# Two of ScalarE's scalings of a token tile placed behind the next tile's square and root

## The chip, the cores and the metric

The kernel runs on one core of one Trainium2 chip. The metric is the device time of one execution in microseconds (us). The kernel before takes 2104.73 us, the median of three runs (2103.9 to 2104.93).

The core has a matrix engine (TensorE, in the profile PE, with PEld for its weight loads), VectorE (DVE), ScalarE (ACT), GpSimd (POOL) and SyncE (SP). The last computes nothing here and issues transfers. ScalarE issues some transfers too; such an issue stands in ScalarE's own instruction order and appears in the trace as ACTq.

## The reference

The reference is one residual decoder block for 512 tokens of width 2048. The change touches only its last lines, in which the gated result of the feed-forward layer is added to the residual stream and the whole row of a token is normalised:

```python
x = x + g2 * jnp.einsum('bsf,fd->bsd', jax.nn.gelu(gate) * val, w_down[l])
return rms_norm(x, norm_final)

def rms_norm(x, g):
    xf = x.astype(jnp.float32)
    y = xf * lax.rsqrt(jnp.mean(xf * xf, axis=-1, keepdims=True) + EPS)
    return (y * g.astype(jnp.float32)).astype(x.dtype)
```

The norm needs the squares of all 2048 columns of a token before any column can be scaled.

## The kernel before

Nearly all of the kernel is one list of steps, each of which multiplies a 512 KB unit of weights. Every fp32 product is made of three matmuls on rounded halves of the operands. The tiles hold features on the 128 partitions and the 512 tokens along the row, up to the last group of the down projection.

The down projection gives 2048 output columns in four groups g = 0 to 3 of 512 columns. Groups 0 to 2 are done in the feature layout. They are added to the residual, weighted with the final norm's gain (`weigh`), transposed on TensorE (`turned`) and kept as `rows[t][g]`: 128 tokens by 512 columns for each of the four token tiles t = 0 to 3. Their sums of squares come from `partial_squares` (`part`). All of that is ready before the end.

Group 3 is computed by tokens, in `group_by_token`. Most of its weight units are multiplied for all four tiles in turn. The last three units are kept back, and their products (six half units, 18 matmuls a tile) are done tile by tile. After tile t's 18 matmuls, `finish(t, ps)` is called:

```python
for t in range(4):
    for m in range(2 * (n - tail), 2 * n):
        mm_h(ps[t], ws[base + m // 2][m % 2], t, lhs[ks[m]], False, m == 2 * n - 1)
    done(t, ps[t])
```

`finish` works so, for one tile (lines of the profile in brackets):

- VectorE multiplies the matmul result by the gate (L1101) and adds the residual (L1102). This is y, the last 512 columns of the row.
- ScalarE squares y and sums along the row into v, one number a token (L1103: an ACTIVATE and an ACTIVATION_READ_ACCUMULATOR).
- VectorE meanwhile multiplies y by the final gain (L1104) and then adds the other columns' mean square to v (L1105).
- ScalarE takes the root (`root`, L105).
- VectorE makes the reciprocal root r in four small instructions (`rsqrt_rest`, L110, L111, L112, L117).
- The four 512-column pieces of the row are multiplied by r and written to `out`, 256 KB each. Piece 3 is done by VectorE (L1110), and pieces 0, 1, 2 by ScalarE (L1112), in that order. In tile 3, VectorE also does piece 1.
- The write of piece 0 is issued by ScalarE, those of the other three by SyncE (L1113).

The instruction order on each engine is the order in which this code runs: an engine does nothing of tile t + 1 before its own part of tile t. When all is written, the end of the program (L1295) waits on SyncE until the writes have landed.

Of the kernel before, what the change touches and what calls it, by code (L numbers as in the profile page):

```python
# [15 lines left out]
P = 128  # L16
S = 512
# [33 lines left out]
def tile_block(ctx, tc, x_t, vec, w_ada, w_in, w_r, w_i, ws_t, w_out, w_up, w_us, w_dn, out):  # L51
    nc = tc.nc
    V, A, G, PE, SY = nc.vector, nc.scalar, nc.gpsimd, nc.tensor, nc.sync
# [7 lines left out]
    def sb(tag, bufs, shape=(P, S), dt=F32, pl=pool):  # L61
        count[0] += 1
        return pl.tile(list(shape), dt, name=f"{tag}_{count[0]}", tag=tag, bufs=bufs)
# [39 lines left out]
    def root(v):  # L103
        s = sb("rsq", 4, (P, 16))[:, :v.shape[1]]
        A.activation(s, v, AF.Sqrt)  # L105
        return s

    def rsqrt_rest(r, v, s, whole=True):
        t = sb("rsq", 4, (P, 16))[:, :v.shape[1]]
        V.reciprocal(s, s)  # L110
        V.tensor_tensor(out=t, in0=s, in1=v, op=MUL)  # L111
        V.tensor_tensor(out=t, in0=t, in1=s, op=MUL)  # L112
        if whole:
            V.tensor_scalar(out=t, in0=t, scalar1=-0.5, scalar2=1.5, op0=MUL, op1=ADD)
            V.tensor_tensor(out=r, in0=s, in1=t, op=MUL)
        else:
            V.scalar_tensor_tensor(out=r, in0=t, scalar=3.0, in1=s, op0=SUB, op1=MUL)  # L117
# [376 lines left out]
    for k in range(KT):  # L494
        if k % 2 == 0:
            both = pair(F32)
        t = both[:, k % 2, :]
# [27 lines left out]
    r = sb("rsr", 2, (P, 4))  # L525
# [569 lines left out]
    def finish(t, ps):  # L1095

        y = rows[t][3]
        q = sb("yl", 4, pl=room2[0])
        v = sb("rsr", 2, (P, 4))[:, 0:1]
        r = sb("rsr", 2, (P, 4))[:, 0:1]  # L1100
        V.tensor_tensor(out=q, in0=ps, in1=across["g2"], op=MUL)  # L1101
        V.tensor_tensor(out=y, in0=q, in1=y, op=ADD)  # L1102
        A.activation(ps, y, AF.Square, scale=D ** -0.5, accum_out=v)  # L1103
        V.tensor_tensor(out=q, in0=y, in1=across["gf"], op=MUL)  # L1104
        V.tensor_tensor(out=v, in0=v, in1=part[0][:, t:t + 1], op=ADD)  # L1105
        rsqrt_rest(r, v, root(v), False)
        for g in (3, 0, 1, 2):
            src = q if g == 3 else rows[t][g]
            if g == 3 or (g == 1 and t == 3):
                V.tensor_scalar(out=src, in0=src, scalar1=r, scalar2=None, op0=MUL)  # L1110
            else:
                A.activation(src, src, AF.Copy, scale=r)  # L1112
            (A if g == 0 else SY).dma_start(out[t * P:(t + 1) * P, g * S:(g + 1) * S], src)  # L1113

    for half in range(2):
        for g in range(4):
            ks = range(HF * half, HF * half + HF)
            srcs = [w_dn[half, g, u] for u in range(HF // 2)]
            if half == 0:
                group(srcs, ks, mm_w, act, down_done(g))  # L1120
            elif g < 3:
                group(srcs, ks, mm_w, act, last_done(g))
            else:
                group_by_token(srcs, ks, act, finish, 3)
# [174 lines left out]
```

## Time and profile before

| | us |
|---|---|
| median of three runs | 2104.73 |
| the profiled execution, its own time | 2104.92 |
| its span, first to last instruction | 2103.2 |
| TensorE matmuls busy | 2069.0 |
| VectorE busy | 1492.9 |
| ScalarE busy | 923.8 |
| last matmul ends | about 2092.3 |
| last scaling ends | about 2099.4 |

Positions are microseconds from the start of the span. The profiled execution's own time is 1.7 us more than its span. The profile lists instructions by engine with start and duration, says what an engine waited for, and follows the work that ended last back to its causes. Transfers have an issue (an instruction of the engine that issues) and a landing. The share of the 16 DMA engines that is busy in a stretch is given beside the rate in GB/s. A bracket at the end of an instruction's row holds the time for which its engine was idle before it, and what ended that.

### The profile page before, as it was taken

The numbers are of one execution on the slowest core, as the hardware profiler recorded it, in microseconds if no ns is written. First come the engines' busy times: TensorE is split into PE (matmuls) and PEld (weight loads), VectorE is DVE, ScalarE is ACT, GpSimd is POOL, SyncE is SP. The second block draws the span as 40 slices with busy tenths as digits, with TensorE's granted clock in tenths as the row PEclk, the third lists the DMA queues.
The fourth block names the chain that finished last, engine by engine and source line by source line (L and its number), as shares of the span: only waits on it lengthen the run. The fifth ranks groups of instructions, "written<-read, shape, count | busy, mean of one in ns | idle before, by whom it ended". The sixth has DMA issues, their size and how long they took to land.

```text
span 2103.2 us, 26309 instructions
## 1 busy us (share of the span) xinstructions
PE 2069.0 (98%) x10160; PEld 1727.6 (82%) x10160; DVE 1492.9 (71%) x1865; ACT 923.8 (44%) x1165; POOL 79.7 (4%) x100
## 2 busy tenths in 40 slices
PE   7999999999989999999999999999999999999997
PEld 4887777888868888888888888888888888888886
DVE  8999889788767888888888888888875223432333
ACT  5323666332234555555555555555553222322223
POOL 0000000000000000000000000000000000000000
PEclk9999999999999999999999999999999999999999
DMA  9977434589825677877877867767755334423222
GB/s 374 327 288 264 141 127 154 199 296 367 298 95 159 212 225 202 241 216 202 242 216 204 240 211 210 248 198 235 216 177 199 121 119 141 159 91 99 92 90 100
DMA packets 116061, 420.36 MB, mean 200 GB/s; under 512 B 14816, under 2 KB 14944, under 8 KB 103648
## 3 DMA queue, kind: packets, MB, share of 16 engines
q1 hardware_dynamic: 87280, 315.39, 42.6%
q0 software_dynamic: 12672, 46.14, 11.6%
q10 hardware_dynamic: 15984, 57.15, 7.9%
q8 instruction: 80, 1.31, 0.2%
q14 instruction: 45, 0.37, 0.0%
HBM read 397.66 MB, written 20.97 MB: 199 GB/s over the span
## 4 chain that ended last, share of the span: by engine, by line
PE 87%; DVE 7%; ACT 3%; issue 1%; DMA 1%; SPq 0%; ACTq 0%; DVEq 0%
PE mm L921 28%; PE mm L922 14%; PE mm L174 13%; PE mm L175 13%; PE mm L176 13%; DVE araw L212 2%; PE mm L181 1%; PE mm L183 1%; PE mm L182 1%; DVE wl L168 1%; DMA araw<-w_ada 1%; DVE xs L359 1%; PE sm L655 0%; DVE la L685 0%; DVE xs L734 0%
## 5 line engine op out<-in xcount | busy, mean ns | idle before, releaser
L163 ACT CAST wh<-raw 128x1024 fp32r<-128x1024 f32 x296 | 311.7, 1053 | 615.1 <-PE mm L175 443.1
L168 DVE TENSOR_TENSOR wl<-raw,wh 128x1024 fp32r<-128x1024 f32 x296 | 360.9, 1219 | 303.8 <-ACT wh L163 303.4
L921 PE MATMUL mm<-hp,wh 128*128 128x512 f32 x1408 | 499.5, 399 | 0.0
L174 PE MATMUL mm<-hp,wh 128*128 128x512 f32 x1184 | 469.0, 396 | 6.7 <-ACT hp L229 5.8
L175 PE MATMUL mm<-hp,wh 128*128 128x512 f32 x1184 | 463.6, 392 | 0.5 <-DVE hp L237 0.5
L176 PE MATMUL mm<-hp,wl 128*128 128x512 f32 x1184 | 462.8, 391 | 0.0
L922 PE MATMUL mm<-hp,wl 128*128 128x256 f32 x1408 | 395.4, 281 | 0.0
L921 PE MATMUL mm<-xs,wh 128*128 128x512 f32 x1056 | 375.1, 399 | 0.0
L921 PEld LDWEIGHTS mm<-hp,wh 128*128 128x128 f32 x1408 | 264.6, 188 | 66.1
L922 PE MATMUL mm<-xs,wl 128*128 128x256 f32 x1056 | 296.6, 281 | 0.0
L174 PEld LDWEIGHTS mm<-hp,wh 128*128 128x128 f32 x1184 | 223.7, 189 | 58.3 <-ACT hp L229 8.7
L922 PEld LDWEIGHTS mm<-hp,wl 128*128 128x128 f32 x1408 | 266.0, 189 | 0.0
L175 PEld LDWEIGHTS mm<-hp,wh 128*128 128x128 f32 x1184 | 223.6, 189 | 50.1 <-issue 2.4
L176 PEld LDWEIGHTS mm<-hp,wl 128*128 128x128 f32 x1184 | 223.6, 189 | 46.6
L168 DVE TENSOR_TENSOR wl<-rawb,wh 128x1024 fp32r<-128x1024 f32 x176 | 214.9, 1221 | 65.6 <-ACT wh L163 65.6
L921 PEld LDWEIGHTS mm<-xs,wh 128*128 128x128 f32 x1056 | 198.4, 188 | 49.6
L922 PEld LDWEIGHTS mm<-xs,wl 128*128 128x128 f32 x1056 | 199.5, 189 | 0.0
L163 ACT CAST wh<-rawb 128x1024 fp32r<-128x1024 f32 x176 | 185.2, 1052 | 23.9 <-PE mm L921 13.3
L212 DVE SCALAR_TENSOR_TENSOR araw<-araw,crow 128x2050 f32<-128x2050 f32 (+1 forms) x80 | 182.6, 2286 | 2.5 <-DMA araw<-w_ada 2.4
L950 POOL DMA_DIRECT2D raw<-w_us x88 | 75.9, 862 | 1240.8 <-DMA rawb<-w_us 457.8
L974 ACT COPY u<-mm 128x512 f32<-128x512 f32 x88 | 51.7, 587 | 161.5 <-PE mm L922 161.5
L168 DVE TENSOR_TENSOR wl<-t,wh 128x1024 fp32r<-128x1024 f32 x44 | 53.9, 1225 | 50.3 <-ACT wh L163 50.3
(233 smaller groups left out, 2106.3 us busy)
## 6 DMA issues: line engine op xcount, KB each, us to landing
rawb<-w_us SPq DMA_DIRECT2D x132, 512.0 KB, 6.8
araw<-w_ada SPq DMA_DIRECT2D x48, 1024.5 KB, 7.6
raw<-w_dn SPq DMA_DIRECT2D x96, 512.0 KB, 3.6
raw<-w_us SPq DMA_DIRECT2D x88, 512.0 KB, 6.2
raw<-w_us POOLq DMA_DIRECT2D x88, 512.0 KB, 7.3
araw<-w_ada SPq DMA_DIRECT2D x32, 1025.0 KB, 8.4
raw<-w_in ACTq DMA_DIRECT2D x59, 512.0 KB, 4.6
yl<-w_ada SPq DMA_DIRECT2D x16, 1024.5 KB, 5.4
```

Of the source, the lines that this page charges most:

```text
L163: A.copy(hi, raw)
L168: V.tensor_tensor(out=lo, in0=raw, in1=hi, op=SUB)
L174: PE.matmul(ps, w[0][:, cs], h[0], start=first, stop=False)
L175: PE.matmul(ps, w[0][:, cs], h[1], start=False, stop=False)
L176: return PE.matmul(ps, w[1][:, cs], h[0], start=False, stop=last)
L181: PE.matmul(ps, h[0][:, cs], w[0], start=first, stop=False)
L182: PE.matmul(ps, h[0][:, cs], w[1], start=False, stop=False)
L212: V.scalar_tensor_tensor(out=raw, in0=raw, scalar=1.0, in1=crow[:, :w], op0=MUL, op1=MUL, accum_out=mods[:, n:n + 1])
L921: PE.matmul(both, hi[:, cs], m, start=first, stop=False, skip_group_check=True)
L922: PE.matmul(ps[:, lower], lo[:, cs], m[:, 0, :], start=False, stop=last, skip_group_check=True)
L950: G.dma_start(o[name], w_us[f - PLAIN, i], accum_op=ADD)
L974: A.copy(t, o["x"])
```

## The change

The change rewrites the end of `finish`. In tiles 0 to 2 only pieces 3 (VectorE) and 2 (ScalarE) are scaled at once. The scalings of pieces 0 and 1, both ScalarE's, are put into a function that runs in the next tile, right behind that tile's root. Tile 3 runs tile 2's two late scalings behind its own root, and then all its own four pieces. The issuing engines change as well: ScalarE now issues the write of piece 2 (in tile 3 those of 0 and 2), and SyncE those of the others. v and r get a tag of their own with four buffers, where they had two shared ones, because r of a tile is read while the next tile's is made.

```diff
-        v = sb("rsr", 2, (P, 4))[:, 0:1]
-        r = sb("rsr", 2, (P, 4))[:, 0:1]
+        v = sb("rsf", 4, (P, 4))[:, 0:1]
+        r = sb("rsf", 4, (P, 4))[:, 0:1]
         V.tensor_tensor(out=q, in0=ps, in1=across["g2"], op=MUL)
         V.tensor_tensor(out=y, in0=q, in1=y, op=ADD)
         A.activation(ps, y, AF.Square, scale=D ** -0.5, accum_out=v)
         V.tensor_tensor(out=q, in0=y, in1=across["gf"], op=MUL)
         V.tensor_tensor(out=v, in0=v, in1=part[0][:, t:t + 1], op=ADD)
-        rsqrt_rest(r, v, root(v), False)
-        for g in (3, 0, 1, 2):
+        s = root(v)
+        if t:
+            late_parts.pop()()
+        rsqrt_rest(r, v, s, False)
+
+        def part_of(g, engine, queue):
             src = q if g == 3 else rows[t][g]
-            if g == 3 or (g == 1 and t == 3):
+            if engine is V:
                 V.tensor_scalar(out=src, in0=src, scalar1=r, scalar2=None, op0=MUL)
             else:
                 A.activation(src, src, AF.Copy, scale=r)
-            (A if g == 0 else SY).dma_start(out[t * P:(t + 1) * P, g * S:(g + 1) * S], src)
+            queue.dma_start(out[t * P:(t + 1) * P, g * S:(g + 1) * S], src)
+
+        def later():
+            part_of(0, A, SY)
+            part_of(1, A, SY)
+
+        if t < 3:
+            part_of(3, V, SY)
+            part_of(2, A, A)
+            late_parts.append(later)
+        else:
+            part_of(3, V, SY)
+            part_of(0, A, A)
+            part_of(1, V, SY)
+            part_of(2, A, A)
+
+    late_parts = []
```

## Rows read from the trace of the kernel before

**Rows 1.** The page: the span, and busy time with share and instructions by engine.

```profile
span 2103.2 us, 26309 instructions
PE 2069.0 (98%) x10160; PEld 1727.6 (82%) x10160; DVE 1492.9 (71%) x1865; ACT 923.8 (44%) x1165; POOL 79.7 (4%) x100
```

**Rows 2.** The chain that ended last, its last links: start, duration, engine, tile, line.

```profile
2094.37 1.33 ACT xs L1112 x2
2095.70 0.62 ACT mm L1103 x2
2097.56 0.73 ACT xs L1112
2098.69 0.72 ACT xs L1112
```

**Rows 3.** ScalarE in order of time, tiles 0 to 2 (start, duration; ACTq is an issue).

```profile
2081.49 0.60 ACT L1103 ACTIVATE mm<-xs 128x512 f32<-128x512 f32 x1 [4.48 <-DVE xs L1102]
...
2082.23 1.28 ACT L105 ACT_TABLE_LOAD   x1
...
2085.30 0.35 ACTq L1113 DMA_DIRECT2D out<-xs  x1
2085.70 1.34 ACT L1112 ACTIVATE xs<-xs,rsr 128x512 f32<-128x512 f32 x2 [0.43 <-ACT xs L1112]
2086.94 0.58 ACT L1103 ACTIVATE mm<-xs 128x512 f32<-128x512 f32 x1
...
2087.87 0.20 ACT L105 ACTIVATE rsq<-rsr 128x1 f32<-128x1 f32 x1 [0.22 <-DVE rsr L1105]
2088.89 0.72 ACT L1112 ACTIVATE xs<-xs,rsr 128x512 f32<-128x512 f32 x1 [0.81 <-DVE rsr L117]
...
2091.29 0.58 ACT L1103 ACTIVATE mm<-xs 128x512 f32<-128x512 f32 x1
```

**Rows 4.** VectorE in order of time, tiles 0 to 2.

```profile
2080.77 0.69 DVE L1102 TENSOR_TENSOR xs<-yl,xs 128x512 f32<-128x512 f32 x1
...
2085.66 0.69 DVE L1102 TENSOR_TENSOR xs<-yl,xs 128x512 f32<-128x512 f32 x1
...
2088.89 0.49 DVE L1110 TENSOR_SCALAR yl<-yl,rsr 128x512 f32<-128x512 f32 x1
2089.29 0.68 DVE L1101 TENSOR_TENSOR yl<-mm,xs 128x512 f32<-128x512 f32 x1
2090.01 0.69 DVE L1102 TENSOR_TENSOR xs<-yl,xs 128x512 f32<-128x512 f32 x1
```

**Rows 5.** TensorE in order of time: the last matmul of tile 3.

```profile
2091.86 0.39 PE L183 MATMUL mm<-wh,dp 128*128 128x512 f32 x1
```

**Rows 6.** ScalarE in order of time, the scalings of tile 3.

```profile
2097.56 0.72 ACT L1112 ACTIVATE xs<-xs,rsr 128x512 f32<-128x512 f32 x1 [0.81 <-DVE rsr L117]
2098.31 0.34 ACTq L1113 DMA_DIRECT2D out<-xs  x1
2098.69 0.72 ACT L1112 ACTIVATE xs<-xs,rsr 128x512 f32<-128x512 f32 x1 [0.42 <-ACT xs L1112]
```

**Rows 7.** SyncE's issues in order of time, tile 3: its first and its last.

```profile
2098.07 0.33 SPq L1113 DMA_DIRECT2D out<-yl  x1
...
2099.44 0.33 SPq L1113 DMA_DIRECT2D out<-xs  x1
```

**Rows 8.** Issues: KB each, us to landing; 2098.07, then 2099.44; then all sixteen.

```profile
out<-yl SPq DMA_DIRECT2D x1, 256.0 KB, 2.1
...
out<-xs SPq DMA_DIRECT2D x1, 256.0 KB, 2.7
...
DMA to landing us min/median/max: 2.0/2.2/3.1
```

**Rows 9.** A stretch of the end: busy time by engine, granted clock, DMA share, GB/s.

```profile
2099.00:2101.50 2.50, 0.00 (x0) 0.00 (x0) 0.00 (x0) 0.41 (x1) 0.00 (x0) 0.50 1.03 386
```

**Rows 10.** Waits of SyncE's queue from 2098: us in total, times, longest.

```profile
SPq L1295 <- DMA out<-xs: 1.9, 3, 0.7
```

## The prediction

> **What bounds the kernel now.** First read the page: TensorE is busy for 2069.0 of a span of 2103.2 us [rows 1]. The change touches nothing of that. It acts only behind the last matmul of a tile, and the last matmul of all ends at 2091.86 + 0.39 = 2092.25 [rows 5], so at most the 11 us from there to the end are at stake, 0.5% of the time. The second view is the chain that ended last: from 2094 on it consists of ScalarE's scalings and squares, one behind another without a gap [rows 2]. So the end is not set by TensorE. It is set by a loop over token tiles, and the third view, ScalarE and VectorE in order of time, shows the loop. Tile 1's square starts at 2086.94 and tile 2's at 2091.29 [rows 3]: 4.35 us a tile. Tile 2's y was ready before that: its addition ran from 2090.01 to 2090.70 [rows 4]. In tile 0, where ScalarE was idle, the square came 0.03 us behind the same addition (2080.77 + 0.69 = 2081.46 against 2081.49) [rows 3, 4]. So 2091.29 - 2090.73 = 0.56 us of each turn is the square waiting for two scalings of the tile before, while VectorE, which needs the root, stands still.
>
> The fourth view is the transfers. In tile 3 the four writes are issued between 2098.07 and 2099.44 [rows 7]. The first lands 2.1 us later, at 2100.17, and the last 2.7 us later, at 2102.14 [rows 8]. Between 2099 and 2101.5 the 16 DMA engines are fully busy, at 386 GB/s [rows 9]. One write of 262144 bytes is 0.68 us at that rate, and the landings agree: (2102.14 - 2100.17) / 3 = 0.66. So the end is a stream of four writes. It begins when the first is issued, and the program's end waits for its last [rows 10].
>
> **The change part by part.**
>
> *The square comes forward.* Tile 1's addition ends at 2085.66 + 0.69 = 2086.35 [rows 4], so its square can start at 2086.38. ScalarE has to be free by then. After r of tile 0 it now does one scaling and one issue, where the row after the issue starts at 2085.70 [rows 3]; that is in time. From square to square the new loop is: square to the next use of r by VectorE, 2088.89 - 2086.94 = 1.95; that to the next gate multiplication, 2089.29 - 2088.89 = 0.40; that to the end of the addition, 2090.01 - 2089.29 + 0.69 = 1.41; and 0.03 to the next square [rows 3, 4]. The sum is 3.79 instead of 4.35. Tile 2's square is then at 2090.17 and tile 3's at 2093.96. By the period of before tile 3's would be at 2086.94 + 2 x 4.35 = 2095.64, so three times 0.56 us, 1.68, are gained. I take r of tile 3 to be used first at 2095.89 instead of 2097.56, 1.67 us earlier [rows 6].
>
> *What else could hold the loop at 3.79.* TensorE: the new gate multiplication of tile 3 comes at 2090.17 + 1.95 + 0.40 = 2092.52, and its last matmul ends at 2092.25 [rows 5]. So TensorE is next in line with 0.27 us to spare. ScalarE: from the square to the root's start is 2087.87 - 2086.94 = 0.93, the root with its gap 0.22, two late scalings 2086.94 - 2085.70 = 1.24 until the next instruction starts [rows 3], then piece 2 with its issue, which I take as long as piece 0 with its issue is now, 2098.69 - 2097.56 = 1.13 [rows 6]. The sum is 3.52 of 3.79: 0.27 us to spare. The late scalings stand where ScalarE waited 0.81 us for r [rows 3]. They end 0.93 + 0.22 + 1.24 = 2.39 us behind the square, r is there at 1.95, and the 0.44 between them delays piece 2 and nothing of VectorE.
>
> *The root.* The root, and then the late pair queued behind it, wait for VectorE's small addition, as the root does now (0.22) [rows 3]. The table load is there once, 1.28 us in tile 0, and none comes between the later squares, roots and scalings [rows 3]. The order of the three kinds changes, the set of kinds does not: I take 0, with 1.28 us as the far end if one load came back.
>
> *The buffers.* Four buffers for v and r mean that r of tile 2 overwrites r of tile 0, which a late scaling reads last. That scaling ends by 2086.38 + 1.15 + 1.34 = 2088.87, and tile 2's r is made at about 2090.17 + 1.9 = 2092.1. The trace of before has no such wait. The lower end is 0; the upper is a wait for the late pair of the running turn, 0.44 us each time. I take 0, since the reader is a whole tile ahead.
>
> *The issues.* An issue costs ScalarE 0.35, and 0.4 with the wait for its own scaling ahead of it [rows 3]. Tiles 0 to 2 keep one each (piece 2 for piece 0). Tile 3 gets a second, behind its last scaling, with nothing queued behind it. On SyncE, tile t's piece 3 now stands behind two late writes of tile t - 1. In tile 3 it is ready at 2095.89 + 0.49 = 2096.38 [rows 4], while the second late piece is ready at 2096.45, so it loses the time of an issue, 0.33 [rows 7]. That is hidden, because the DMA engines still have the late writes to move.
>
> *The end.* Root of tile 3 starts at 2093.96 + 0.93 = 2094.89; late piece 0 at 2095.11, ends 0.72 later at 2095.83; its write is issued at 2095.86. Late piece 1 ends at about 2096.45. Tile 3's piece 0 starts at 2095.11 + 1.24 = 2096.35, and its issue and the last scaling follow as now, the scaling 1.13 us after (2098.69 - 2097.56) [rows 6]: from 2097.48 to 2098.20, issued at 2098.23. That is 1.21 us ahead of the 2099.44 of before [rows 7].
>
> But the last stream now has six writes instead of four, since tile 2's two late pieces are in it. It starts 2098.07 - 2095.86 = 2.21 us earlier and is two writes, 1.36 us, longer. By rows: 2095.86 + 2.1 = 2097.96 for the first landing, and five more at 0.66 to 0.68 put the last at 2101.26 to 2101.36, where it is 2102.14 now [rows 8, 9]. The net is 0.78 to 0.88 us; I take 0.85, the difference of 2.21 and 1.36. Of 1.67 us won at r, half goes into the two writes that have become late.
>
> The sum on the profiled execution is 2104.92 - 0.85 = 2104.07. It lies 0.19 above the median of the three runs, so I predict a median of 2103.9.
>
> One rule speaks of the size of a write. The Trainium skill ("DMA: Bandwidth & Descriptors", Specifications) puts HBM's share of one core at about 358 GB/s. By that a write would be 0.73 us, an estimate, and the last landing 0.25 us later. The row of this kernel, 386 GB/s, is above that figure, and the sum goes by the row.
>
> **The rivals.**
>
> *The last issue decides, not the stream.* If the six writes move without queueing, the end is the last issue plus one landing: 2098.23 + 2.1 to 2.7 = 2100.3 to 2100.9, a gain of 1.2 to 1.8 us, and a median near 2103.2. For it: the last issue does come 1.21 us earlier. Against it: the engines are already full with four writes [rows 9], and the longest landing is 3.1 us against 2.0 for the shortest [rows 8]. Two of the six would have to pass in no time.
>
> The Trainium skill ("Trainium Kernel Development and Optimization", Key Constraints) says that transfers issued by SP, ACT and POOL share the same 16 DMA engines, so that a second issuing engine saves only time of issue. By that this rival has no ground, and the busy share of this trace agrees.
>
> *It does not do what it says.* The square is held by something other than the two scalings, and the writes are spread as they are today: no change, median 2104.7. Against it: tile 0, in which the square follows the addition by 0.03 us with nothing ahead of it [rows 3].
>
> *Slower: the two late pieces at the very end cost more than the loop gives back.* Its place is tile 3's root. Whatever the loop gains, two scalings and two writes of tile 2 now stand behind that root. Were the period still 4.35, late piece 0 would start 2095.11 + 1.67 = 2096.78, its write would be issued at 2097.53, and six writes would land by 2097.53 + 2.1 + 5 x 0.67 = 2102.98: 0.84 us later than now, a median of 2105.6. It decides once the loop gains less than half of the 1.67 us, so less than 0.28 a tile. TensorE or ScalarE would have to be late by over 0.5 us a turn for that, and each has 0.27 to spare.
>
> **How the numbers follow.** The forecast has a chance of 0.62 (2103.9, give or take 0.5 for the spread of the runs of before). The rival by the last issue has 0.14 (2103.2), no change 0.10 (2104.7), the slower one 0.10 (2105.6). All lie within 0.2% (4.2 us), which is about what a measurement of this kernel can tell from no change. The remaining 0.04 goes to something far from this tile loop, on either side by more than 4.2 us. So: faster 0.02, within 0.2% 0.96, slower 0.02. The range has to leave out no more than 2 in 10. It goes from 2102.6, the gain of 1.8 us less a little of the runs' spread, to 2105.2, which takes in no change with its spread; most of the slower rival lies above it.
>
> **What would show it.** In the changed kernel's trace, squares should come 3.8 us apart and start 0.03 us behind the addition, with ScalarE idle before them. The late pair should follow the root at once. Piece 2 should start about 0.44 us after r. The DMA engines should be full without a gap for six writes, 6 x 0.68 = 4.1 us, at the end. The last landing should be near 2101.3 and the span near 2102.35. I am wrong if squares are still over 4.1 us apart, if gate multiplications wait for TensorE, if the last write lands within 2.2 us of its issue, or if a second table load shows.

## The result, and the profile after

The changed kernel takes 2120.3 us, the median of four runs (2120.18 to 2120.71), against 2104.41 us of the kernel before measured with it (2103.9 to 2104.93). The ratio is 1.0075 with a 95% interval of 1.0061 to 1.0089. It is slower by about 16 us, where 0.8 us less was forecast, and lies far outside the range given.

The page of the changed kernel, first its span and its busy time by engine:

```profile
span 2119.0 us, 26309 instructions
...
PE 2089.3 (99%) x10160; PEld 1733.6 (82%) x10160; DVE 1495.2 (71%) x1865; ACT 921.8 (44%) x1165; POOL 79.9 (4%) x100
```

The number of instructions is the same on each engine as in [rows 1]. TensorE's matmuls, of which the change touches none, are busy for 20.3 us more (2089.3 against 2069.0). The mean granted clock of TensorE is 0.993 in both executions, so this is not the clock.

Next, the tile loop that the change rewrites. VectorE's first multiplication of each of the four tiles, in order of time:

```profile
2096.88 0.69 DVE L1101 TENSOR_TENSOR yl<-mm,xs 128x512 f32<-128x512 f32 x1 [1.89 <-PE mm L183]
...
2101.79 0.68 DVE L1101 TENSOR_TENSOR yl<-mm,xs 128x512 f32<-128x512 f32 x1
...
2105.61 0.69 DVE L1101 TENSOR_TENSOR yl<-mm,xs 128x512 f32<-128x512 f32 x1
...
2109.43 0.68 DVE L1101 TENSOR_TENSOR yl<-mm,xs 128x512 f32<-128x512 f32 x1
```

The same rows of tiles 0 and 1 in the kernel before; its tile 2 has the 2089.29 of [rows 4]:

```profile
2080.04 0.69 DVE L1101 TENSOR_TENSOR yl<-mm,xs 128x512 f32<-128x512 f32 x1 [1.77 <-PE mm L183]
...
2084.95 0.68 DVE L1101 TENSOR_TENSOR yl<-mm,xs 128x512 f32<-128x512 f32 x1
```

Tiles 1 to 3 are now 3.82 us apart, where tile 2 stood 4.34 behind tile 1. The loop does what the forecast said. But its first row is at 2096.88 instead of 2080.04: the loop begins 16.84 us late. From that row to the end of the span it is 2119.0 - 2096.88 = 22.12 us, and was 2103.2 - 2080.04 = 23.16: the loop is 1.04 us shorter, and everything lost was lost ahead of it.

ScalarE in that loop, tiles 1 and 2 of the changed kernel (the row x3 is the late pair and piece 2, one behind another):

```profile
2103.24 0.60 ACT L1103 ACTIVATE mm<-xs 128x512 f32<-128x512 f32 x1 [1.12 <-DVE xs L1102]
2103.78 0.19 ACT L1103 ACTIVATION_READ_ACCUMULATOR mm<-xs 128x1 f32 x1
2104.19 0.20 ACT L105 ACTIVATE rsq<-rsf 128x1 f32<-128x1 f32 x1 [0.23 <-DVE rsf L1105]
2104.30 1.94 ACT L1116 ACTIVATE xs<-xs,rsf 128x512 f32<-128x512 f32 x3
2106.27 0.35 ACTq L1117 DMA_DIRECT2D out<-xs  x1
2107.05 0.60 ACT L1103 ACTIVATE mm<-xs 128x512 f32<-128x512 f32 x1 [0.82 <-DVE xs L1102]
```

Against [rows 3] the square no longer stands behind scalings. ScalarE is idle for 0.82 us before it, and what ends the wait is VectorE's addition.

Where the time went shows in the groups of matmuls by operands. A matmul multiplies a moving tile with weights, which have a load of their own (PEld). Each line names the moving tile first, then the weights, the count, busy us and mean ns of one. `wh` and `wl` are a unit of weights, rounded, and the rest that rounding leaves; `hp`, `xs` and `dp` hold activations in the same two parts. In the up projection's split steps (L921 and L922) the tokens are taken by halves of 256: a 512-column matmul takes both parts of a half, a 256-column one its rounded part. All other steps have three 512-column matmuls for each product. First the kernel before:

```profile
L921 PE MATMUL mm<-hp,wh 128*128 128x512 f32 x1408 | 499.5, 399 | 0.0
...
L176 PE MATMUL mm<-hp,wl 128*128 128x512 f32 x1184 | 462.8, 391 | 0.0
L922 PE MATMUL mm<-hp,wl 128*128 128x256 f32 x1408 | 395.4, 281 | 0.0
...
L183 PE MATMUL mm<-wh,hp 128*128 128x512 f32 x192 | 74.9, 390 | 0.0
...
L176 PE MATMUL mm<-dp,wl 128*128 128x512 f32 x160 | 62.3, 389 | 0.0
...
L176 PE MATMUL mm<-xs,wl 128*128 128x512 f32 x64 | 24.9, 389 | 0.0
```

And the changed kernel:

```profile
L921 PE MATMUL mm<-hp,wh 128*128 128x512 f32 x1408 | 496.3, 394 | 0.0
...
L176 PE MATMUL mm<-hp,wl 128*128 128x512 f32 x1184 | 469.4, 396 | 0.0
L922 PE MATMUL mm<-hp,wl 128*128 128x256 f32 x1408 | 398.5, 283 | 0.0
...
L183 PE MATMUL mm<-wh,hp 128*128 128x512 f32 x192 | 75.8, 395 | 0.0
...
L176 PE MATMUL mm<-dp,wl 128*128 128x512 f32 x160 | 62.3, 390 | 0.0
...
L176 PE MATMUL mm<-xs,wl 128*128 128x512 f32 x64 | 25.3, 395 | 0.0
```

In the steps with three products, every group that has `hp` or `xs` on either side is 5 to 6 ns slower per matmul. The same instruction on `dp` is not. The pairs of a 512- and a 256-column matmul in the split steps change the other way: 5 ns less and 2 ns more.

Laying the starts of the matmuls of both executions side by side, one by one in program order, gives the sum. Where the split steps begin, the changed kernel is 11.7 us behind; where they end, 6.3; at the last matmul, 17.1. So it loses 11.7 and 10.9 us in the steps with three products, 22.6 in all, and wins 5.5 in the split steps.

What these operands have in common is where they lie. In the compiled programs, `hp`, `raw` and `xs` stand 128 bytes a partition lower than before, as the pool that holds them grew by the four 32-byte buffers of `rsf` while the two of `rsr` stay in use elsewhere. `wh`, `wl` and `dp` lie in pools at the other side and have not moved. In the kernel before, `hp`, `xs` and `dp` all stand at a multiple of 512 bytes from the weights.

### The profile page after: what moved, and what is told of

Its sections match the earlier page's. It is cut to its first block, busy times and chain, and to the rows that moved or that the text cites. A ratio compares the mean times of both kernels' runs of the same rounds, so it can differ in the third digit from the quotient of the medians.

```text
span 2119.0 us, 26309 instructions
## 1 busy us (share of the span) xinstructions
PE 2089.3 (99%) x10160; PEld 1733.6 (82%) x10160; DVE 1495.2 (71%) x1865; ACT 921.8 (44%) x1165; POOL 79.9 (4%) x100
## 4 chain that ended last, share of the span: by engine, by line
PE 91%; DVE 5%; ACT 2%; issue 1%; DMA 1%; SPq 0%; ACTq 0%; DVEq 0%
PE mm L921 27%; PE mm L922 14%; PE mm L175 14%; PE mm L176 14%; PE mm L174 14%; PE mm L181 2%; PE mm L183 2%; PE mm L182 2%; DVE araw L212 1%; DVE wl L168 1%; PE sm L129 1%; DVE xs L359 0%; PE sm L655 0%; DVE xs L734 0%; PE sm L176 0%
## 5 line engine op out<-in xcount | busy, mean ns | idle before, releaser
L921 PE MATMUL mm<-hp,wh 128*128 128x512 f32 x1408 | 496.3, 394 | 0.0
L176 PE MATMUL mm<-hp,wl 128*128 128x512 f32 x1184 | 469.4, 396 | 0.0
L922 PE MATMUL mm<-hp,wl 128*128 128x256 f32 x1408 | 398.5, 283 | 0.0
L921 PE MATMUL mm<-xs,wh 128*128 128x512 f32 x1056 | 372.6, 394 | 0.0
L921 PEld LDWEIGHTS mm<-hp,wh 128*128 128x128 f32 x1408 | 264.4, 188 | 60.8
L922 PE MATMUL mm<-xs,wl 128*128 128x256 f32 x1056 | 298.9, 283 | 0.0
L922 PEld LDWEIGHTS mm<-hp,wl 128*128 128x128 f32 x1408 | 265.0, 188 | 0.0
L921 PEld LDWEIGHTS mm<-xs,wh 128*128 128x128 f32 x1056 | 198.3, 188 | 45.6
L922 PEld LDWEIGHTS mm<-xs,wl 128*128 128x128 f32 x1056 | 198.7, 188 | 0.0
```

The costliest lines, as they stand in the source:

```text
L176: return PE.matmul(ps, w[1][:, cs], h[0], start=False, stop=last)
L921: PE.matmul(both, hi[:, cs], m, start=first, stop=False, skip_group_check=True)
L922: PE.matmul(ps[:, lower], lo[:, cs], m[:, 0, :], start=False, stop=last, skip_group_check=True)
```

## The experiments

Two theories: **placement** (matmuls whose moving tile and weights stand at another distance run slower) and **order** (something in the new instruction order slows the whole program).

### The four buffers alone

```diff
-        v = sb("rsr", 2, (P, 4))[:, 0:1]
-        r = sb("rsr", 2, (P, 4))[:, 0:1]
+        v = sb("rsf", 4, (P, 4))[:, 0:1]
+        r = sb("rsf", 4, (P, 4))[:, 0:1]
```

> The kernel before with one edit: v and r of the last tiles come from the tag rsf with four buffers. No instruction changes its place. The four buffers of 32 bytes move the pool's tiles hp, raw and xs by 128 bytes a partition; the weight tiles wh and wl stay. Theory of placement (matmuls whose two operands stand 128 bytes off each other against before run slower): the last tile's first gate multiplication comes some 17 us later, hp with wh takes 395 ns instead of 389, and the time is 2104.4 + 16.9 = 2121.3 us. Theory of order (the new instruction order slows the whole): 2104.4 us, all durations as before.

It took 2121.27 us against 2104.69 of the kernel before measured with it, ratio 1.0075 (1.006 to 1.009): the whole loss, without a moved instruction. Its matmuls, and its first multiplications by the gate in tiles 0, 2 and 3:

```profile
L176 PE MATMUL mm<-hp,wl 128*128 128x512 f32 x1184 | 468.9, 396 | 0.0
...
L176 PE MATMUL mm<-dp,wl 128*128 128x512 f32 x160 | 62.3, 390 | 0.0
```

```profile
2095.52 0.69 DVE L1101 TENSOR_TENSOR yl<-mm,xs 128x512 f32<-128x512 f32 x1 [1.89 <-PE mm L183]
...
2104.77 0.68 DVE L1101 TENSOR_TENSOR yl<-mm,xs 128x512 f32<-128x512 f32 x1
...
2109.11 0.68 DVE L1101 TENSOR_TENSOR yl<-mm,xs 128x512 f32<-128x512 f32 x1
```

The tiles are 4.34 us apart, as before the change, and the loop begins 15.5 us late. The theory of order falls.

### The new order without the move

The changed kernel with more buffers, so that the tiles move by 512 bytes:

```diff
-        v = sb("rsf", 4, (P, 4))[:, 0:1]
-        r = sb("rsf", 4, (P, 4))[:, 0:1]
+        v = sb("rsf", 16, (P, 4))[:, 0:1]
+        r = sb("rsf", 16, (P, 4))[:, 0:1]
```

> The changed kernel with sixteen buffers of rsf instead of four, so that hp, raw and xs move by 512 bytes. Theory of placement, if what counts is the distance of the two operands up to a multiple of 512 bytes: matmuls as before (389 ns), and only the new order's gain is left, 1.0 us, 2103.4 us. Theory of order: 2120.3 us as in the changed kernel. If any displacement costs: 2120 us or more.

It took 2103.84 us against 2104.69, ratio 0.9993 (0.9984 to 1.0002). The matmuls are those of the kernel before:

```profile
L921 PE MATMUL mm<-hp,wh 128*128 128x512 f32 x1408 | 499.5, 399 | 0.0
...
L176 PE MATMUL mm<-hp,wl 128*128 128x512 f32 x1184 | 463.2, 391 | 0.0
```

The loop is that of the changed kernel. The first multiplications by the gate in tiles 0, 2 and 3:

```profile
2079.73 0.69 DVE L1101 TENSOR_TENSOR yl<-mm,xs 128x512 f32<-128x512 f32 x1 [1.77 <-PE mm L183]
...
2088.45 0.68 DVE L1101 TENSOR_TENSOR yl<-mm,xs 128x512 f32<-128x512 f32 x1
...
2092.26 0.68 DVE L1101 TENSOR_TENSOR yl<-mm,xs 128x512 f32<-128x512 f32 x1
```

From the first of these to the end of its span of 2102.0 us it is 22.27 us, 0.89 less than before. The forecast gain of the order is there. It is too small for the timed runs to part it from no change; in the trace it is plain.

### Distance or address

If the distance of the two operands counts, moving both must be harmless, and moving the weights alone must cost as much as moving `hp`. Both kernels have the order of the kernel before. The first has `rsf` of four buffers (`hp` 128 bytes lower) and a pad that raises the lower pools by 384 bytes; the second has only a pad of 128 bytes (32 elements instead of the 96 shown):

```diff
+    wpad = wts.tile([P, 96], F32, name="wpad")
+    V.memset(wpad, 0.0)
```

> The kernel before with rsf of four buffers, so that hp, raw and xs stand 128 bytes lower, and a pad of 384 bytes ahead of the weights, so that all tiles of the lower pools stand 384 bytes higher: the distance of hp to wh changes by 512 bytes, while each of them stands at another multiple of 128. Theory that the distance counts: 2104.4 us, hp with wh 389 ns. Theory that hp's own address counts: 2121 us. The order of work is that of the kernel before.

It took 2105.18 us, ratio 1.0 (0.999 to 1.0009).

> The kernel before with a pad of 128 bytes ahead of the weights: wh, wl and the other tiles of the lower pools, dp among them, move, hp and xs stay. Theory that the distance counts: hp with wh is off by 128 bytes as in the changed kernel, 395 ns and 2121 us, while dp with wh stays at 390 ns. Theory that hp's own address counts: 2104.4 us.

It took 2121.35 us, ratio 1.0076 (1.006 to 1.0093). The group of `hp` with `wl`, in the first and in the second:

```profile
L178 PE MATMUL mm<-hp,wl 128*128 128x512 f32 x1184 | 463.0, 391 | 0.0
```

```profile
L178 PE MATMUL mm<-hp,wl 128*128 128x512 f32 x1184 | 469.3, 396 | 0.0
...
L178 PE MATMUL mm<-dp,wl 128*128 128x512 f32 x160 | 62.3, 390 | 0.0
```

In the second, `hp` has not moved and is slow; `dp` has moved together with the weights and is not. The distance counts, not the address.

### Other distances

The four-buffer experiment again, with eight buffers (256 bytes) and with two (64 bytes).

> The kernel before with v and r from a tag rsf of eight buffers: hp, raw and xs move by 256 bytes against the weights, no instruction changes its place. If the distance counts only up to a multiple of 256 bytes: 2104.4 us, hp with wh 389 ns. If it counts up to a multiple of 512 (the one multiple tried so far): another duration than 389 ns, and a time between that of the kernel before and twice the loss of the 128-byte move, 2104 to 2138 us.

2105.09 us against 2104.86, ratio 1.0 (0.9989 to 1.0012): 256 bytes are free, and the group of `hp` with `wl` has its duration of before:

```profile
L176 PE MATMUL mm<-hp,wl 128*128 128x512 f32 x1184 | 462.6, 391 | 0.0
```

> The same with two buffers: hp, raw and xs move by 64 bytes. If the loss comes with any displacement that is no multiple of the period: 395 ns and about 2121 us. If it grows with the displacement: half of the loss at 128 bytes, 392 ns and about 2113 us. If less than 128 bytes is harmless: 2104.4 us.

2128.54 us, the median of two runs, ratio 1.0112 (1.0082 to 1.0141). This is outside all three expectations: half the displacement costs more than the whole. Its groups show why:

```profile
L921 PE MATMUL mm<-hp,wh 128*128 128x512 f32 x1408 | 499.5, 397 | 0.0
...
L176 PE MATMUL mm<-hp,wl 128*128 128x512 f32 x1184 | 469.3, 396 | 0.0
L922 PE MATMUL mm<-hp,wl 128*128 128x256 f32 x1408 | 395.6, 281 | 0.0
```

The three-product steps lose about as much as with 128 bytes, and the busy time of the split steps stays at 499.5 and 395.6, so that the gain there, 5.5 us with 128 bytes, is missing. Matmul by matmul, it is 13.8 us behind at the split steps' beginning and still 13.8 at their end.

### All distances in one execution

The weights of each step are put at another offset within longer buffers; everything else is as before:

```diff
-    def round_up(raw):
-        hi = sb("wh", WBUFS, (P, 2, S), F32R, wts)
+    def room_for(tag, off):
+        t = sb(tag, WBUFS, (P, 2 * S + 64), F32R, wts)
+        return t[:, off:off + 2 * S].rearrange("p (a b) -> p a b", a=2)
+
+    def round_up(raw, off):
+        hi = room_for("wh", off)
...
+    def offset(j):
+        return 8 * (j % 8)
```

(`rest` does the same for `wl`; `off` is the offset of step j, in elements of four bytes.)

> The kernel before, with the rounded weights of each step placed at another offset in their buffers (0 to 224 bytes in steps of 32 over eight steps, and buffers 256 bytes farther apart), so that one execution holds all distances of weights and moving tile in steps of 32 bytes up to 512. Read by matmul, not by its time. If the distance alone counts: start-to-start intervals fall into classes by distance, 226.7 ns at 0 and about 232 ns at 128 bytes below, in the three-product steps; in the steps of 512- and 256-column matmuls the pair is 353.4 ns at 0 and 351.2 ns at 128 bytes. If the address of the weights counts too: one distance shows two intervals, by which buffer holds the weights.

The kernel took 2122.79 us in its one run; what counts is the interval by matmul. The table gives the mean time from a matmul's start to the next one's start, for `hp` as the moving tile. Intervals above 300 ns are left out. The table is worked out from the trace's 9920 matmuls on rounded operands, put beside the program's list of them with their addresses. The distance is the moving tile's address less that of the weights that the next matmul uses, modulo 256 bytes. Within a step the matmul's own weights stand at the same distance. Where one step follows another, one of the two can be at 0 without the other: in the three-product steps the interval is then 227 ns (the median of 25) with the next weights at 0, and 235 (of 23) with only its own there. That speaks for the next weights, on few cases.

| distance, bytes | three-product steps, ns | split steps: 512 columns + 256 columns, ns |
|---|---|---|
| 0 | 227.2 | 235.6 + 116.7 = 352.3 |
| 32 | 233.3 | 229.0 + 118.0 = 347.0 |
| 64 | 229.6 | 229.8 + 118.8 = 348.6 |
| 96 | 233.4 | 235.8 + 119.7 = 355.5 |
| 128 | 233.1 | 231.4 + 120.6 = 352.0 |
| 160 | 233.8 | 229.8 + 117.2 = 347.0 |
| 192 | 233.2 | 233.9 + 118.2 = 352.1 |
| 224 | 233.2 | 234.7 + 118.3 = 353.0 |

Distances 256 bytes apart agree: taken modulo 512, 128 and 384 give 233.1 and 233.1 in the three-product steps, 32 and 288 give 233.4 and 233.2. `xs` and `dp` give the same as `hp` within 0.6 ns at each distance at which there are more than two of them. The whole kernels agree with the table in the three-product steps (227.0 before, 232.9 after). In the split steps they have 353.3 and 351.1 at 0 and 128, about 1 ns off the 352.3 and 352.0 here; that is not explained. A move of `hp` by 64 bytes down is distance 192, and the table gives for it what was measured: 6 ns more in the three-product steps, nothing in the split steps. So the distance modulo 256 bytes decides, and the two kinds of steps have different best places. The three-product steps are best at 0, where the kernel before had them. The split steps are better at 32, 64 and 160 than at 0, by 3.7 to 5.3 ns a pair within this run.

### A placement for each kind of step

So the order of the changed kernel, the tiles at 256 bytes (`rsf` with eight buffers), and an offset in the split steps alone (those in `source`), of 56 elements or 224 bytes in one kernel and 24 elements or 96 bytes in the other:

```diff
+    def offset(j):
+        return 56 if j in source else 0
```

> The changed kernel's order of work, rsf with eight buffers (a move of 256 bytes), and in the up projection's 308 split steps alone the rounded weights stand 224 bytes into buffers that are 256 bytes longer, so that the moving tile is 32 bytes ahead of the weights up to a multiple of 256; all other steps stay at 0. From the sweep: the pair of a 512- and a 256-column matmul takes 347.0 ns there against 353.3 in the kernel before. Theory of distance: 2464 pairs by 6.3 ns are 15.5 us less, 2103.8 - 15.5 = 2088.3 us. If the sweep's intervals were owed to the change of offset from step to step, and not to the distance: 2103.8 us.

2088.15 us against 2105.99, ratio 0.9909 (0.9891 to 0.9927).

> The same with 96 bytes instead of 224: the moving tile is 160 bytes ahead. The sweep has 347.0 ns for the pair here too. Theory of distance: 2088.3 us. If only a small distance helps: 2103.8 us.

2086.65 us, ratio 0.9904 (0.9887 to 0.9922). Both beat both kernels, 17.8 and 19.3 us under the kernel before on the same chip. The split steps of the second one:

```profile
L928 PE MATMUL mm<-hp,wh 128*128 128x512 f32 x1408 | 490.1, 392 | 0.0
...
L180 PE MATMUL mm<-hp,wl 128*128 128x512 f32 x1184 | 462.8, 391 | 0.0
L929 PE MATMUL mm<-hp,wl 128*128 128x256 f32 x1408 | 393.5, 280 | 0.0
```

Here the three-product steps have the 391 ns of the kernel before, and the 512-column matmuls of the split steps have 392 instead of 399. Matmul by matmul it gains 16.4 us between the beginning and the end of the split steps, 2464 pairs by 6.7 ns, where 6.3 ns were expected.

## Why the prediction was wrong

**The step that failed is the one on the buffers.** It reads "Four buffers for v and r mean that r of tile 2 overwrites r of tile 0", looks for a wait, finds none, and takes 0 between 0 and 0.44 us a turn. As to waits that holds: no row of the loop waits for a buffer. But buffers also take room, and the step did not ask what the room moves. The four buffers alone cost the whole loss, 16.6 us in the first experiment (2121.27 against 2104.69). With it fell the opening, that the change touches nothing of TensorE's 2069.0 us and that at most 11 us are at stake. The trace of before could not have given the price, since there every pair stands at distance 0. That `hp` and `xs` would move could have been read from the program.

**The loop was right.** Measured from the first gate multiplication, so that the late beginning drops out (2080.04 before, 2096.88 after):

| | forecast | measured |
|---|---|---|
| square to square | 3.79 | 3.81 and 3.82 (2103.24, 2107.05, 2110.87) |
| first use of r in tile 3 | 2095.89, 15.85 behind | 2112.84, 15.96 behind |
| last scaling starts | 2097.48, 17.44 behind | 2114.28, 17.40 behind |
| last write issued | 2098.23, 18.19 behind | 2115.03, 18.15 behind |
| last landing | 2101.26 to 2101.36, at most 21.32 behind | 2115.03 + 3.0 = 2118.03, 21.15 behind |
| gain from there to the end of the span | 0.85 | 1.04, and 0.89 without the move |

**One size was off within it.** The late pair was set 0.22 us behind the root's start; it follows at 0.11 (2104.19 and 2104.30), as the root and the first scaling overlap. So ScalarE is through with the pair about a tenth of a microsecond earlier than forecast. VectorE sets the period, so nothing came of that.

**One reading was wrong, and nothing rests on it.** The prediction calls the end of the chain "scalings and squares, one behind another without a gap". [rows 2] show 1.24 us between the square's end (2095.70 + 0.62 = 2096.32) and the next scaling at 2097.56, in which the trace has ScalarE's root and VectorE's small instructions, and 0.40 us ahead of the last scaling.

**The stream of six writes was right**, and the rival by the last issue fell. The last issue and its landing, and a stretch of the end, in the changed kernel:

```profile
2115.03 0.34 ACTq L1117 DMA_DIRECT2D out<-xs  x1
```

```profile
out<-xs ACTq DMA_DIRECT2D x1, 256.0 KB, 3.0
```

```profile
2113.50:2116.50 3.00, 0.00 (x0) 0.00 (x0) 0.22 (x1) 1.08 (x2) 0.00 (x0) 0.50 1.04 400
```

The last write lands 3.0 us behind its issue, where a write with nothing ahead of it took 2.1 [rows 8]. The DMA engines are full, here at 400 GB/s. The first use of r in tile 3 gained 1.56 us (17.52 behind the first gate multiplication before, 15.96 now), and 1.59 without the move; the end gained 1.04 and 0.89. So a third to under half of it went into the two late writes, where about half was worked out. The 358 GB/s that the forecast took from the Trainium skill ("DMA: Bandwidth & Descriptors", Specifications) are below both rates that the rows show, 386 and 400.

**The slower rival fell too.** Its condition was that the loop gains under half of the 1.67 us, and it gained 1.56. The kernel is slower, but not by that mechanism. The truth lay in the 0.04 left for "something far from this tile loop", of which the slower side had 0.02. The range was built from the loop alone.

**What stays open** is what in the chip makes the distance matter. That the reads of the moving tile and the loads of the next weights disturb each other at some distances would fit a period in bytes and the effect being mutual, but it is only argued. The Trainium skill ("TensorE: Matmul & The Clock Gate", Step-by-step: what each phase is for) says that TensorE reads the streaming operand and the weights over two independent ports, so that loading the next weights takes nothing from the running matmul. That alone gives no ground for the distance to matter. The runs show 227 to 234 ns by distance within one execution (mean granted clock 0.992), and the measurement decides; whether the ports are the place of it, no run here shows.

## What to carry to other kernels

A new buffer is also a displacement of its neighbours: before a small edit is priced at its own place, compare the addresses of the tiles that the busiest engine reads, in the two programs, and hold them with a pad where they should not move. When a time changes by more than the edited stretch can hold, compare the mean durations of the same instruction by operands ahead of that stretch; an operand that has not moved (here `dp`) is the control. And where TensorE bounds a kernel, the distance of its two operands is worth trying for each kind of step apart, as it can be changed by an offset without any other edit.

## What the runs showed of the hardware

In this kernel the start-to-start time of 512-column matmuls on rounded fp32 operands depends on the distance of moving tile and weights in a partition, modulo 256 bytes: 227 ns at 0, 230 at 64, and 233 to 234 at the other multiples of 32. For alternating 512- and 256-column matmuls it is the pair that varies, from 347.0 ns at 32 and 160 to 355.5 at 96, with 352.3 at 0. Either operand may be the one that is moved. Over this kernel that is from 2086.65 us (split steps at 160, the rest at 0, about 1 us of it by the new order) to 2128.54 us (`hp`, `raw` and `xs` moved by 64), 2% of the time, with the same instructions on TensorE.
